# A recurrent mixer with its score blocks stored head innermost, turned by fours, and multiplied on 128 rows

## The chip, the cores and the metric

The program runs on one core of a Trainium2 chip. The core has five engines that work from queues of their own: TensorE (PE in the profile; the loads of its stationary operand are listed as PEld), VectorE (DVE), ScalarE (ACT), GpSimd (POOL) and SyncE (SP), which issues the transfers here. The metric is the device time in microseconds (us) of one execution, and its median over the runs.

## The reference, cut to what matters

The reference is a block of four parts in a row (a gated mixer, a recurrent mixer, a second mixer with attention, and feed-forward layers between them) on 256 tokens of width 1024. The change touches the recurrent mixer alone, which has 16 heads of 64:

```python
kk = heads(k * k_k)
kk = kk / jnp.maximum(jnp.sqrt(jnp.sum(kk * kk, axis=-1, keepdims=True)), 1e-12)
k = k * (1 + (a - 1) * k_a)
...
y = wkv7_scan(rh, decay, kh, vh, -kk, kk * ah)

def step(state, inp):
    r_t, w_t, k_t, v_t, a_t, b_t = inp
    sa = jnp.einsum('bhvk,bhk->bhv', state, a_t)
    state = (state * w_t[:, :, None, :] + sa[..., None] * b_t[:, :, None, :]
             + v_t[..., None] * k_t[:, :, None, :])
    return state, jnp.einsum('bhvk,bhk->bhv', state, r_t)
...
bonus = jnp.sum(rh * kh * r_k.astype(f32), axis=-1, keepdims=True) * vh
y = (y + bonus.reshape(bsz, seq, d)).astype(h.dtype)
return (y * g) @ w_o, v_first
```

## The kernel before, in words

The recurrence over 256 tokens is done in four chunks of 64 tokens. For each chunk `c` and head there is a 128x128 block of scores: the rows are the chunk's tokens seen through `b` and `k` (`BK`), the columns are its tokens seen through `a` and `r` (`AR`). `scores(c, g)` computes eight heads' blocks (`g` is the half of the heads) with TensorE into two banks, one for even heads (`sce`) and one for odd ones (`sco`), and VectorE multiplies them by a mask into `SC[g]`. `SC[g]` holds, on 128 partitions, 32 blocks (four chunks by eight heads) by 2 halves (`x`: 0 for the `a` columns, 1 for the `r` columns) by 64 columns, in this order: a block's columns lie side by side.

Within a chunk the first 64x64 part `A` of each block has to be inverted as a triangular system. It is split in 32x32 blocks. `by_problems(g)` turns the two diagonal blocks of each problem with 128 small matmul instructions against an identity (`turn`, bank `rb`), so that `Ab` has one problem per partition (128 problems: 2 halves, 2 diagonal blocks, 32 chunk-and-head pairs) and the 32x32 numbers of it along the row. `Ab` is divided by the squared norms of the keys. These are summed by TensorE (`squares`, bank `ssps`, 16 rows by 256 tokens), and `norms()` moves them with 16 transfers on SP's queue to `pd`, one problem per partition; their reciprocal is `ip`. `solve(s)`, 31 steps on VectorE, computes the inverses into `Xb`. `Ab` and `Xb` are the two halves of the tile `ABX`.

The inverses go back in two forms: into `SC` (bank `xt`, `turn` on 64 rows) and into `X1` (bank `x1`, `turn` on 32 rows). Then come 64 products of 32x32 with 32 rows each (bank `q`), copied into `X1`, and 64 more of 32x32 (bank `x21`), copied into the corner of each block of `SC`. The trace writes some names without their digits: the rows of `x` with `cstt,ABX` are `x1`, those with `SC,X` are `x21`, and `X` is `X1`.

The loop over the chunks then multiplies with these blocks: `removals` (bank `W`), `U`, the state's update `S` and the output `Y`. Each of `W`, `U` and `Y` takes one head's 64 columns of `SC` as the stationary operand; even heads go to the upper and odd heads to the lower 64 rows of the bank. `UV` holds the results on its upper 64 partitions and the values `v`, shifted by their mean (`ms`, `mv`, added by POOL), on the lower 64.

Beside this, on TensorE, there are the products for the values (`values`, bank `v`, `v0` and `v1` for the two halves of the columns, eight steps each), for the gates (`gates`, bank `g`), the turns of `BK` (`by_tokens`, bank `bkt`), the coefficients of the bonus (`coefs`, bank `cf`, 128 columns loaded and 2 streamed), the turn of the bonus (`bonus`, bank `bon`) and of the gates (`gate_turn`, bank `gt`).

A framework allots the buffers, places the waits and chooses the order on each engine from the order of the program, priorities and its own estimate of times. So TensorE's order is not always that of the source: a `v` step can stand ahead of a turn that was written before it. Every matmul of 32-bit floats appears in the trace as two instructions with a load each; the counts below are of instructions.

Of the kernel before, what the change touches and what calls it, by code (L numbers as in the profile page):

```python
# [9 lines left out]
F32 = mybir.dt.float32  # L10
# [48 lines left out]
for _n, _c in _PVL:  # L59
# [6 lines left out]
    ("ident", 128), ("ones", 128), ("onec", 1), ("bones", 128), ("invf", 1), ("hind", 128),  # L66
# [9 lines left out]
def consts():  # L76
# [13 lines left out]
    hi = np.zeros((P, 8, 16), np.float32)  # L90
    for m in range(8):
        hi[p, m, 2 * m + p // 64] = 1.0
    put("hind", hi.reshape(P, 128))
# [169 lines left out]
class Kern:  # L263
# [96 lines left out]
    def turn(self, out, a, rows):  # L360

        self.mm(out, a, self.cst("ident", 128)[rows, rows])

# [9 lines left out]
    def busy(self, n):  # L373

        o = self.cst("ones", 128).bitcast(BF16)
        ps = self.bank("busy")
        for _ in range(n):
            self.mm(ps[:, 0:T], o[:, 0:P], o)

# [373 lines left out]
    def rwkv(self, sums, nxt):  # L753
# [147 lines left out]
        ssps = []  # L901
# [21 lines left out]
        def squares(j, sq):  # L923
            if not ssps:
                ssps.append(self.bank("ssps"))
            for m in range(2):
                mm = 2 * j + m
                self.mm(ssps[0][0:16, 0:T], self.cst("hind", 128)[:, mm * 16:(mm + 1) * 16], sq[:, m, :], mm == 0, mm == 7)

        pd = self.tiny("pd", [P, 32], tag="pd")  # L930

        def norms():
            ss = self.mid("ss16", (16, T))
            self.ts(ss, ssps[0][0:16, 0:T], 1e-24, 2.0, ALU.max, ALU.mult)
            for b in range(2):
                for g in range(2):
                    for c in range(4):
                        p0 = 64 * g + 32 * b + 8 * c
                        nc.sync.dma_start(out=pd[p0:p0 + 8, :],
                                          in_=ss[8 * g:8 * g + 8, c * 64 + b * 32:c * 64 + b * 32 + 32])  # L940
# [25 lines left out]
        SC = [pair("SC")[:, 0:4096].rearrange("p (i x t) -> p i x t", i=32, x=2) for _ in range(2)]  # L966
        tri = self.cst("tri", 128)

        def scores(c, g):
# [6 lines left out]
            for par in range(2):  # L976
                o = SC[g][:, 8 * c + par:8 * c + 8:2, :, :].rearrange("p a x t -> p a (x t)")
# [12 lines left out]
        def by_problems(g):  # L990

            for e in range(2):
                ps = self.bank("rb")
                for i in range(16):
                    for b in range(2):
                        q = slice(32 * b, 32 * b + 32)
                        self.turn(ps[q, i * 32:(i + 1) * 32], SC[g][q, :, 0, 32 * b + 16 * e + i], q)
# [1112 lines left out]
```

## Time and profile before

| | |
|---|---|
| median of 3 runs | 1151.2 us (1149.26 to 1152.41) |
| the profiled execution | 1150.61 us, span of its instructions 1148.8 us |
| mean granted TensorE clock | 0.974 |
| TensorE busy | 1098.6 us (96%), 9220 matmul instructions |
| VectorE busy | 852.0 us (74%) |
| ScalarE busy | 574.9 us (50%) |
| POOL busy | 188.5 us (16%) |
| read from memory | 199.98 MB, 175 GB/s over the span |

The span runs from the first to the last instruction of the core. An engine is busy while one of its instructions runs; matmuls overlap each other, so their durations add up to more than the time they take together. The granted clock is a share of TensorE's full 2.4 GHz. The recurrent mixer lies at about 270 to 480 us of the span.

### The profile page before, as it was taken

The page shows a single profiled execution, that of the slowest core. Times are in us where ns is not written, and L with a number is a line of the kernel's source. Part 1 is how long each engine was busy: PE and PEld are TensorE (multiplying, and loading weights), DVE is VectorE, ACT ScalarE, POOL GpSimd, SP SyncE. Part 2 cuts the span into 40 slices and gives each one's busy share as a digit, 9 for nine tenths or more (in the row PEclk, how much of TensorE's full clock was granted, in tenths as well). Part 3 has the DMA queues.
Part 4 walks back from the last instruction along what each step waited for, and adds up shares of the span by engine and source line. Part 5 has one row for each costly group of instructions (what it writes and reads, how often), then busy time and mean ns, then how long its engine had stood idle before and what let it go on. Part 6 is the DMA issues. An engine that isn't in the chain of part 4 may idle for free. (4 is left out here: it accounts for less than half of the span.)

```text
span 1148.8 us, 22642 instructions
## 1 busy us (share of the span) xinstructions
PE 1098.6 (96%) x9220; PEld 1032.4 (90%) x9220; DVE 852.0 (74%) x1552; ACT 574.9 (50%) x922; POOL 188.5 (16%) x137
## 2 busy tenths in 40 slices
PE   9799999999999999999999998899899997999997
PEld 7699999999887598999999998897798997999886
DVE  6878988547954846888975579799886958965444
ACT  5565444444731545654454546454545654755342
POOL 1310000002010021110000004776363014000000
PEclk9999999999998979999999999899899998999999
DMA  8468887653441310588865543444144542555552
GB/s 291 152 206 306 302 297 281 209 183 126 136 142 59 132 38 21 184 302 314 281 206 184 182 164 130 151 164 132 67 135 157 172 162 92 179 186 169 187 189 82
DMA packets 57817, 202.52 MB, mean 176 GB/s; under 512 B 6896, under 2 KB 8560, under 8 KB 57712
## 3 DMA queue, kind: packets, MB, share of 16 engines
q1 hardware_dynamic: 57712, 201.07, 51.7%
q8 instruction: 72, 1.18, 0.4%
q14 instruction: 33, 0.27, 0.1%
HBM read 199.98 MB, written 1.05 MB: 175 GB/s over the span
## 5 line engine op out<-in xcount | busy, mean ns | idle before, releaser
L185 ACT ACTIVATE hi<-raw 128x1024 fp32r<-128x1024 f32 (+1 forms) x310 | 322.5, 1048 | 265.2 <-PE ps L355 175.2
L186 DVE TENSOR_TENSOR lo<-raw,hi 128x1024 fp32r<-128x1024 f32 (+1 forms) x258 | 315.4, 1226 | 145.3 <-ACT hi L185 144.9
L355 PE MATMUL ps<-xl,hi 128*128 128x256 f32 x1104 | 313.9, 285 | 4.1 <-DVE xl L343 4.1
L355 PE MATMUL ps<-xh,hi 128*128 128x256 f32 x1104 | 316.1, 287 | 1.4 <-ACT hi L185 1.0
L355 PE MATMUL ps<-xh,lo 128*128 128x256 f32 x1104 | 311.8, 283 | 2.8 <-DVE lo L186 1.5
L355 PEld LDWEIGHTS ps<-xl,hi 128*128 128x128 f32 x1104 | 210.4, 191 | 5.4 <-DVE xl L343 5.0
L355 PEld LDWEIGHTS ps<-xh,lo 128*128 128x128 f32 x1104 | 210.3, 191 | 4.4 <-DVE lo L186 3.0
L355 PEld LDWEIGHTS ps<-xh,hi 128*128 128x128 f32 x1104 | 209.7, 190 | 3.5 <-ACT hi L185 2.3
L186 POOL TENSOR_TENSOR lo<-raw,hi 128x1024 fp32r<-128x1024 f32 x52 | 126.0, 2442 | 115.6 <-ACT hi L185 75.9
L343 DVE SCALAR_TENSOR_TENSOR cva<-up,cwh,cva 128x256 f32<-128x256 f32 x232 | 103.3, 483 | 3.2 <-ACT cva L352 1.1
L355 PE MATMUL ps<-zl,hi 128*128 128x256 f32 x352 | 99.6, 283 | 0.0
L355 PE MATMUL ps<-zh,lo 128*128 128x256 f32 x352 | 99.4, 282 | 0.0
L355 PE MATMUL ps<-zh,hi 128*128 128x256 f32 x352 | 98.7, 280 | 0.0
L254 POOL TENSOR_TENSOR sq<-sq 128x512 f32<-128x512 f32 x17 | 23.3, 1374 | 453.2 <-ACT sq L352 453.0
L343 DVE SCALAR_TENSOR_TENSOR ada<-ada,cb 128x1024 f32<-128x1024 f32 x48 | 58.6, 1222 | 16.7 <-DMA ada<-in_ada_dram 16.6
L355 PEld LDWEIGHTS ps<-zh,hi 128*128 128x128 f32 x352 | 66.9, 190 | 0.0
L355 PEld LDWEIGHTS ps<-zh,lo 128*128 128x128 f32 x352 | 66.1, 188 | 0.0
L355 PEld LDWEIGHTS ps<-zl,hi 128*128 128x128 f32 x352 | 65.8, 187 | 0.0
L355 PE MATMUL ps<-hi,zl 128*128 128x256 f32 (+1 forms) x160 | 56.1, 350 | 0.0
L355 PE MATMUL ps<-hi,zh 128*128 128x256 f32 (+1 forms) x160 | 56.0, 350 | 0.0
L355 PE MATMUL ps<-lo,zh 128*128 128x256 f32 (+1 forms) x160 | 55.9, 350 | 0.0
L352 ACT ACTIVATE s<-z 128x256 f32<-128x256 f32 x44 | 18.3, 417 | 71.2 <-DVE z L340 71.1
(438 smaller groups left out, 2260.8 us busy)
## 6 DMA issues: line engine op xcount, KB each, us to landing
raw<-in_w_dram SPq DMA_DIRECT2D x325, 512.0 KB
ada<-in_ada_dram SPq DMA_DIRECT2D x48, 512.0 KB
h<-in_x_dram SPq DMA_DIRECT2D x8, 128.0 KB
cb<-in_c_dram SPq DMA_DIRECT2D x2, 512.0 KB
out_dram<-ht SPq DMA_DIRECT2D x3, 256.0 KB
raw<-in_w_dram SPq DMA_DIRECT2D x2, 256.0 KB
cstt<-in_cst_dram SPq DMA_DIRECT2D x1, 448.5 KB
poolw<-in_poolw_dram SPq DMA_DIRECT2D x1, 256.0 KB
```

What stands on the lines that cost most here:

```text
L185: self.nc.scalar.activation(out=hi[:, s], in_=raw[:, s], func=AF.Copy)
L186: eng.tensor_tensor(out=lo[:, s], in0=raw[:, s], in1=hi[:, s].bitcast(F32), op=ALU.subtract)
L254: e.tensor_tensor(out=self.parts[0], in0=self.parts[0], in1=self.parts[-1], op=ALU.add)
L343: self.nc.vector.scalar_tensor_tensor(out=out, in0=a, scalar=s, in1=b, op0=op0, op1=op1, **k)
L352: self.nc.scalar.activation(out=out, in_=a, func=f, **k)
L355: self.nc.tensor.matmul(out=out, lhsT=lhsT, rhs=rhs, start=start, stop=stop, skip_group_check=True)
```

## The change

The scores are stored in another order, `SC[g]` as 2 halves by 64 columns by 32 chunk-and-head pairs, so that the pairs are innermost. `by_problems` then turns four columns by 32 pairs at a time, with 128 rows and 128 columns, into one bank. `squares` adds its sums straight into the layout of `pd`, with 32-column windows of a constant (`hwin`), so that `norms()` and its transfers go. `Ab` is divided in two halves, each after its own turn. The inverses are turned by `first_block` (into `X1`) and by `blocks` (both diagonal blocks, by fours). `below` and `corner` are the two rounds of products, now with all 128 rows (zeros in `X1` and in the new tile `Q` fill the rest) and two heads at a time into different rows of one bank. Half of the steps of `v1` are placed between these rounds; before, all came ahead of them. The sums, the copies and the bonus of the first half of `v` move ahead of them. The second `corner` round, the turns of the bonus (`bonus_turn`) and of the gates move into the loop over the chunks. The first `removals` uses only the lower 64 rows. Eight matmuls without use (`busy_on`) are added ahead of the last normalised turn.

```diff
@@ -87,10 +87,9 @@
     put("invf", invf[p % 32][:, None])
-    hi = np.zeros((P, 8, 16), np.float32)
-    for m in range(8):
...
+    hi = np.zeros((P, 64), np.float32)
+    hi[p, 32 + p // 64] = 1.0
+    put("hwin", hi)
     s = (p % 64)[:, None]
@@ -376,6 +371,12 @@
             self.mm(ps[:, 0:T], o[:, 0:P], o)
+    def busy_on(self, n, src):
+        ps = self.bank("busy")
+        for _ in range(n):
+            self.mm(ps[:, 0:P], self.cst("ones", 128), src)
@@ -921,23 +922,19 @@
         def squares(j, sq):
-            if not ssps:
-                ssps.append(self.bank("ssps"))
+            if not pdps:
+                pdps.append(self.bank("pd"))
             for m in range(2):
                 mm = 2 * j + m
-                self.mm(ssps[0][0:16, 0:T], self.cst("hind", 128)[:, mm * 16:(mm + 1) * 16], sq[:, m, :], mm == 0, mm == 7)
+                for b in range(2):
+                    q = 64 * (mm // 4) + 32 * b
+                    for c in range(4):
+                        o = 8 * c + 2 * (mm % 4)
+                        self.mm(pdps[0][q:q + 32, 0:32], self.cst("hwin", 64)[:, 32 - o:64 - o],
+                                sq[:, m, 64 * c + 32 * b:64 * c + 32 * b + 32], mm % 4 == 0 and c == 0, mm % 4 == 3 and c == 3)
...
         pd = self.tiny("pd", [P, 32], tag="pd")
-        def norms():
-            ss = self.mid("ss16", (16, T))
...
@@ -963,7 +960,7 @@
-        SC = [pair("SC")[:, 0:4096].rearrange("p (i x t) -> p i x t", i=32, x=2) for _ in range(2)]
+        SC = [pair("SC")[:, 0:4096].rearrange("p (x t i) -> p x t i", i=32, x=2) for _ in range(2)]
         tri = self.cst("tri", 128)
@@ -974,7 +971,7 @@
             for par in range(2):
-                o = SC[g][:, 8 * c + par:8 * c + 8:2, :, :].rearrange("p a x t -> p a (x t)")
+                o = SC[g][:, :, :, 8 * c + par:8 * c + 8:2].rearrange("p x t a -> p a (x t)")
                 iv = pss[par].rearrange("p (a t) -> p a t", a=4)
@@ -989,17 +986,21 @@
-            for e in range(2):
-                ps = self.bank("rb")
...
+            ps = self.bank("rb")
+            for b in range(2):
+                for e in range(8):
+                    o = 32 * b + 4 * e
+                    self.mm(ps[:, b * T + 32 * e:b * T + 32 * e + 32],
+                            SC[g][:, 0, o:o + 4, :].rearrange("p t h -> p (t h)"), self.cst("ident", 128)[:, 32 * b:32 * b + 32])
+            for q in range(4):
+                for b in range(2):
+                    p0 = 64 * g + 32 * b
+                    o = Ab[p0:p0 + 32, q:32:4, :]
+                    iv = ps[32 * q:32 * q + 32, b * T:b * T + T].rearrange("p (a s) -> p a s", a=8)
+                    if g == 1 and q % 2:
+                        nc.vector.tensor_copy(out=o, in_=iv)
+                    else:
+                        self.act(o, iv, AF.Copy)
@@ -1011,12 +1012,14 @@
                     self.mm(ps[:, 16 * tt + 2 * m:16 * tt + 2 * m + 2], rk[:, m, tt * P:(tt + 1) * P],
-                            self.cst("hind", 128)[:, 0:2])
+                            self.cst("hwin", 64)[:, 32:34])
             self.act(cf.rearrange("p a b -> p (a b)"), ps[:, 0:32], AF.Copy)
...
+        bos = {}
         def bonus(n):
...
-            bo = self.hlp.tile([P, 2, 512], F32, tag=("hi", "lo")[n], name="bo")
+            bo = bos[n] = self.hlp.tile([P, 2, 512], F32, tag=("hi", "lo")[n], name="bo")
             for tt in range(2):
@@ -1025,12 +1028,15 @@
                     self.act(bo[:, tt, q], psv[tt][n][:, q], AF.Copy, scale=cf[:, tt, hh:hh + 1])
+        def bonus_turn(n):
             for j in (2 * n, 2 * n + 1):
...
                         o = (m % 2) * T + tt * P
-                        self.tr(ps[:, o:o + P], bo[:, tt, (m % 4) * P:(m % 4 + 1) * P], P)
+                        self.tr(ps[:, o:o + P], bos[n][:, tt, (m % 4) * P:(m % 4 + 1) * P], P)
                 for m in (2 * j, 2 * j + 1):
@@ -1106,15 +1112,20 @@
         scores(1, 1)
-        norms()
+        self.ts(pd, pdps[0][:, 0:32], 1e-24, 2.0, ALU.max, ALU.mult)
+        nc.vector.reciprocal(out=ip, in_=pd)
+        nc.vector.tensor_copy(out=Xb.rearrange("p a b -> p (a b)")[:, 0:1024:33], in_=ip)
         scores(2, 1)
...
             rkk(j)
-        nc.vector.reciprocal(out=ip, in_=pd)
-        nc.vector.tensor_copy(out=Xb.rearrange("p a b -> p (a b)")[:, 0:1024:33], in_=ip)
+        def divided(g):
+            q = slice(64 * g, 64 * g + 64)
+            self.tt(Ab[q], Ab[q], ip[q].unsqueeze(2).to_broadcast([64, 32, 32]), ALU.mult)
+        divided(0)
         by_problems(1)
-        self.tt(Ab, Ab, ip.unsqueeze(2).to_broadcast([P, 32, 32]), ALU.mult)
+        divided(1)
         for s in range(31):
@@ -1151,74 +1162,110 @@
         coefs()
-        for i in range(8):
-            next(v1)
...
         self.dump("Xb", ABX)
...
             nc.gpsimd.memset(u[0:64, :, :], 0.0)
-        def copied(o, iv, g):
-            if g == 0:
+        ms, mv = self.tiny("ms", [P, 2, 16], tag="cf", bufs=3), self.tiny("mv", [P, 4, 16], tag="mv", bufs=1)
+        def means(n):
+            for tt in range(2):
+                nc.vector.tensor_reduce(out=ms[:, tt, 8 * n:8 * n + 8], in_=psv[tt][n].rearrange("p (a b) -> p a b", a=8),
+                                        axis=AX.X, op=ALU.add)
+        def upper(n):
+            for c in range(4):
+                o, iv = UV[c // 2][64:128, c % 2, n * 512:(n + 1) * 512], psv[c // 2][n][64 * (c % 2):64 * (c % 2) + 64, :]
+                self.act(o, iv, AF.Copy)
+        def copied(o, iv, e):
+            if e % 2 == 0:
                 nc.vector.tensor_copy(out=o, in_=iv)
...
-        X1 = self.xp.tile([64, 2, 32, 32], F32, tag="xl", name="X1")
-        for e in range(4):
+        X1 = self.xp.tile([P, 2, 32, 32], F32, tag="xl", name="X1")
+        nc.gpsimd.memset(X1, 0.0)
+        block = lambda b: self.cst("ident", 128).rearrange("p (g b h) -> p b g h", g=2, b=2)[:, b]
+        by_col = lambda ps, q: ps[32 * q:32 * q + 32, :].rearrange("p (e a) -> p a e", e=8)
+        def first_block():
+            ps = self.bank("x1")
+            for e in range(8):
+                for q in range(4):
+                    self.mm(ps[32 * q:32 * q + 32, 64 * e:64 * e + 64], Xb[:, :, 4 * e + q], block(0))
+            for q in range(4):
+                copied(X1[0:32, :, :, q:32:4].rearrange("p g h e -> p (g h) e"), by_col(ps, q), q)
+        def blocks(b):
             ps = self.bank("xt")
-            for i in range(8):
+            for e in range(8):
+                self.mm(ps[:, 64 * e:64 * e + 64], Xb[:, 4 * e:4 * e + 4, :].rearrange("p t s -> p (t s)"), block(b))
+            return ps
+        def blocks_out(b, ps):
+            for q in range(4):
                 for g in range(2):
-                    self.turn(ps[32 * g:32 * g + 32, i * 64:(i + 1) * 64], Xb[64 * g:64 * g + 64, 8 * e + i, :], slice(64 * g, 64 * g + 64))
-            for b in range(2):
...
+                    copied(SC[g][32 * b:32 * b + 32, 0, 32 * b + q:32 * b + 32:4, :],
+                           ps[32 * q:32 * q + 32, :].rearrange("p (e g h) -> p g e h", e=8, g=2)[:, g], g)
+        Q = {}
+        rows = lambda par: slice(64 * par, 64 * par + 64)
+        def below(cp):
+            ps = self.bank("q")
+            for i in range(16):
+                for par in range(2):
+                    g, ch = i // 8, 16 * cp + 2 * (i % 8) + par
+                    self.mm(ps[64 * par + 32:64 * par + 64, 32 * i:32 * i + 32], SC[g][:, 0, 32:64, ch], X1[:, g, ch, :])
+            for par in range(2):
+                copied(Q[0][32:64, :, 16 * cp + par:16 * cp + 16:2, :],
+                       ps[64 * par + 32:64 * par + 64, :].rearrange("p (g a t) -> p g a t", g=2, a=8), par)
+        def corner(cp):
+            ps = self.bank("x21")
+            for i in range(16):
+                for par in range(2):
+                    g, ch = i // 8, 16 * cp + 2 * (i % 8) + par
+                    self.mm(ps[64 * par:64 * par + 32, 32 * i:32 * i + 32], Q[0][:, g, ch, :], SC[g][:, 0, 32:64, ch])
             for g in range(2):
-                ps = self.bank("q")
-                for i in range(16):
...
+                for par in range(2):
+                    copied(SC[g][0:32, 0, 32:64, 16 * cp + par:16 * cp + 16:2].rearrange("p t a -> p a t"),
+                           ps[64 * par:64 * par + 32, T * g:T * g + T].rearrange("p (a t) -> p a t", a=8), par)
+        for i in range(4):
+            next(v1)
+            if i == 1:
+                bonus(0)
+                upper(0)
+                means(0)
+        first_block()
+        xt = [blocks(b) for b in (1, 0)]
+        Q[0] = self.slot("Q", (P, 2, 32, 32))
+        nc.gpsimd.memset(Q[0], 0.0)
+        blocks_out(1, xt[0])
+        next(v1)
+        next(v1)
+        below(0)
+        next(v1)
+        below(1)
+        next(v1)
+        blocks_out(0, xt[1])
+        corner(0)
+        means(1)
         for c in range(4):
             self.act(mv[64:128, c, :], ms[64 * (c % 2):64 * (c % 2) + 64, c // 2, :], AF.Copy, scale=-1.0 / 64)
-        for c in range(4):
-            for n in range(2):
...
+        upper(1)
         for c in range(4):
...
         bonus(1)
-        gate_turn()
@@ -1275,10 +1321,12 @@
             pss = [self.bank("W") for _ in range(2)]
+            q = slice(64, P) if c == 0 else slice(0, P)
             for g in range(2):
                 for i, par in ips:
-                    self.mm(pss[g][rows(par), vcol(i)], SC[g][:, 8 * c + 2 * i + par, 0, :],
-                            UV[c // 2][:, c % 2, vcol(8 * g + 2 * i + par)], i == 0, c == 0)
+                    self.mm(pss[g][rows(par), vcol(i)], SC[g][q, 0, :, 8 * c + 2 * i + par],
+                            UV[c // 2][q, c % 2, vcol(8 * g + 2 * i + par)], i == 0, c == 0)
             return pss
@@ -1305,7 +1353,7 @@
                     for i, par in ips:
-                        self.mm(ps[rows(par), vcol(i)], SC[g][:, 8 * c + 2 * i + par, 0, :], W[:, 8 * g + 2 * i + par, :])
+                        self.mm(ps[rows(par), vcol(i)], SC[g][:, 0, :, 8 * c + 2 * i + par], W[:, 8 * g + 2 * i + par, :])
                     copy_out(uvh, g, ps)
@@ -1319,6 +1367,8 @@
                         self.tt(o, iv, dcb, ALU.mult)
+            if c == 0:
+                corner(1)
             if c < 3:
@@ -1328,7 +1378,7 @@
                 for i, par in ips:
-                    self.mm(ps[rows(par), vcol(i)], SC[g][:, 8 * c + 2 * i + par, 1, :], uv[:, vcol(8 * g + 2 * i + par)],
+                    self.mm(ps[rows(par), vcol(i)], SC[g][:, 1, :, 8 * c + 2 * i + par], uv[:, vcol(8 * g + 2 * i + par)],
                             c == 0 and i == 0, True)
@@ -1341,7 +1391,11 @@
                 self.act(sq[g][y0:y0 + 64], o, AF.Square)
+            if c == 0:
+                bonus_turn(0)
+                bonus_turn(1)
             if c == 1:
+                gate_turn()
                 gn(0, sq, (nc.gpsimd, nc.gpsimd))
@@ -1366,6 +1420,7 @@
             if m == 6:
+                self.busy_on(8, sq[1][:, 0:P])
                 gated(0)
...
             gated(j)
```

## Rows read from the trace of the kernel before

**Rows 1.** Stretches: length, busy us (count) of PE, PEld, DVE, ACT, POOL; clock; DMA.
```profile
365.00:372.00 7.00, 7.00 (x58) 6.94 (x53) 0.00 (x0) 0.59 (x1) 0.00 (x0) 0.53 0.27 89
372.00:387.00 15.00, 15.00 (x91) 11.03 (x89) 14.40 (x72) 6.27 (x13) 0.00 (x0) 1.00 0.41 135
...
401.70:410.80 9.10, 8.26 (x257) 7.63 (x256) 6.23 (x13) 6.50 (x17) 8.59 (x6) 1.00 0.37 126
...
412.00:426.00 14.00, 14.00 (x237) 13.58 (x233) 2.73 (x4) 3.91 (x8) 0.00 (x0) 0.52 0.01 2
426.00:452.20 26.20, 25.77 (x673) 23.17 (x672) 17.45 (x45) 14.01 (x35) 1.63 (x2) 1.00 0.07 22
452.20:460.80 8.60, 5.59 (x49) 5.13 (x45) 7.37 (x19) 6.70 (x16) 5.22 (x6) 0.97 0.02 5
460.80:464.00 3.20, 3.20 (x16) 3.20 (x17) 3.08 (x10) 1.50 (x4) 0.00 (x0) 0.55 0.58 164
```

**Rows 2.** Timeline of PE: start us, duration us, instructions, count.
```profile
362.07 3.87 PE L355 MATMUL rb<-cstt,SC 32*32 32x32 f32 x128
365.88 7.38 PE L355 MATMUL g<-raw,xg 128*128 128x160 f32 x32
373.09 1.04 PE L358 MATMUL bkt<-cstt,BK 128*128 128x128 f32 x8
...
383.46 3.63 PE L355 MATMUL cf<-cstt,rk 128*128 128x2 f32 x32
386.95 7.11 PE L355 MATMUL v<-raw,xv 128*128 128x512 f32 x16
393.90 1.04 PE L358 MATMUL bon<-cstt,bo 128*128 128x128 f32 x8
394.77 7.03 PE L355 MATMUL v<-raw,xv 128*128 128x512 f32 x16
...
410.83 5.70 PE L355 MATMUL q<-X,SC 32*32 32x32 f32 x125 [0.87 <-DVE X L1167]
...
423.27 1.97 PE L358 MATMUL bon<-cstt,bo 128*128 128x128 f32 x8
...
426.02 1.20 PE L355 MATMUL W<-UV,SC 128*64 128x64 f32 x32
...
433.46 1.11 PE L355 MATMUL U<-W,SC 128*64 128x64 f32 x31
```

**Rows 3.** Timeline of DVE around the solve, 372 to 397.
```profile
372.06 0.35 DVE L1114 RECIPROCAL ip<-pd 128x32 f32<-128x32 f32 x1 [7.26 <-DMA raw<-in_w_dram]
372.52 0.20 DVE L1115 COPY ABX<-ip 128x32 f32<-128x32 f32 x1
372.91 1.22 DVE L340 TENSOR_TENSOR ABX<-ABX,ip 128x1024 f32<-128x1024 f32 x1 [0.19 <-issue]
...
396.79 0.19 DVE L340 TENSOR_TENSOR ABX<-ABX,tb 128x31 f32<-128x31 f32 x1
```

**Rows 4.** Groups by line and form, 322 to 480: busy us, mean ns, idle before.
```profile
L340 DVE TENSOR_TENSOR SC<-sce,cstt 128x512 f32<-128x512 f32 x8 | 5.5, 686 | 9.3 <-PE sco L355 9.3
...
L1167 DVE COPY SC<-xt 32x256 f32<-32x256 f32 x8 | 3.3, 412 | 1.8 <-ACT SC L352 1.3 <-PE xt L355 0.3
```

**Rows 5.** Stretch of tile q alone: PE, PEld, DVE, ACT, clock, DMA.
```profile
411.00:412.00 1.00, 1.00 (x37) 1.00 (x35) 0.00 (x0) 0.00 (x0) 1.00 0.06 16
```

**Rows 6.** Loads of four tiles: ns min/median/max, first and last start us.
```profile
L355 PEld LDWEIGHTS rb<-cstt,SC x256: 127/145/148, 348.5 to 365.7; 32*32 32x32 f32 x128
...
L355 PEld LDWEIGHTS xt<-cstt,ABX x128: 102/107/107, 401.7 to 408.7; 64*32 64x32 f32 x128
...
L355 PEld LDWEIGHTS q<-X,SC x128: 101/152/153, 410.8 to 416.4; 32*32 32x32 f32 x128
...
L355 PEld LDWEIGHTS U<-W,SC x128: 132/138/138, 427.3 to 448.4; 128*64 128x64 f32 x128
```

**Rows 7.** Timeline of POOL, 400 to 411.
```profile
402.84 7.48 POOL L1219 TENSOR_TENSOR UV<-UV,mv 64x1024 f32<-64x1024 f32 x4
```

More of the change, by code (lines that the diff above doesn't have):

```diff
@@ L65 @@
 _CL = [
-    ("ident", 128), ("ones", 128), ("onec", 1), ("bones", 128), ("invf", 1), ("hind", 128),
+    ("ident", 128), ("ones", 128), ("onec", 1), ("bones", 128), ("invf", 1), ("hwin", 64),
     ("tri", 128), ("reset", 256), ("perm", 128), ("cmask", 128),
@@ L358, in tr @@
         self.nc.tensor.transpose(out, a, self.cst("ident", 128)[p0:p0 + n, p0:p0 + n])
-    def turn(self, out, a, rows):
-        self.mm(out, a, self.cst("ident", 128)[rows, rows])
     def warm(self):
@@ L900, in rwkv @@
         kps = {}
-        ssps = []
+        pdps = []
         def keys(j):
@@ L990, in by_problems @@
         def by_problems(g):
-            for e in range(2):
-                ps = self.bank("rb")
-                for i in range(16):
-                    for b in range(2):
-                        q = slice(32 * b, 32 * b + 32)
-                        self.turn(ps[q, i * 32:(i + 1) * 32], SC[g][q, :, 0, 32 * b + 16 * e + i], q)
-                o = Ab[64 * g:64 * g + 64, 16 * e:16 * e + 16, :].rearrange("p a b -> p (a b)")
-                if e == 0 and g == 1:
-                    nc.vector.tensor_copy(out=o, in_=ps[0:64, :])
-                else:
-                    self.act(o, ps[0:64, :], AF.Copy)
+            ps = self.bank("rb")
[13 more added lines that the diff above has]
+                        self.act(o, iv, AF.Copy)
         ip = self.tiny("ip", [P, 32], tag="pd")
@@ L1153, in rwkv @@
         coefs()
-        for i in range(8):
-            next(v1)
-            if i == 3:
-                bonus(0)
         self.dump("Xb", ABX)
@@ L1169, in copied @@
                 self.act(o, iv, AF.Copy)
-        X1 = self.xp.tile([64, 2, 32, 32], F32, tag="xl", name="X1")
-        for e in range(4):
-            ps = self.bank("xt")
-            for i in range(8):
-                for g in range(2):
-                    self.turn(ps[32 * g:32 * g + 32, i * 64:(i + 1) * 64], Xb[64 * g:64 * g + 64, 8 * e + i, :], slice(64 * g, 64 * g + 64))
-            for b in range(2):
-                for g in range(2):
-                    copied(SC[g][32 * b:32 * b + 32, :, 0, 32 * b + 8 * e:32 * b + 8 * e + 8],
-                           ps[32 * g:32 * g + 32, :].rearrange("p (i b c) -> p b c i", i=8, b=2)[:, b], g)
-            if e % 2 == 0:
-                ps1 = self.bank("x1")
-            for i in range(8):
-                for g in range(2):
-                    o = (8 * (e % 2) + i) * 32
-                    self.turn(ps1[32 * g:32 * g + 32, o:o + 32], Xb[64 * g:64 * g + 32, :, 8 * e + i], slice(64 * g, 64 * g + 32))
-            if e % 2:
-                for g in range(2):
-                    copied(X1[0:32, g, :, 8 * e - 8:8 * e + 8], ps1[32 * g:32 * g + 32, :].rearrange("p (i c) -> p c i", i=16), g)
@@ L1190, in rwkv @@
-        for e in range(2):
-            for g in range(2):
-                ps = self.bank("q")
-                for i in range(16):
-                    ch = 16 * e + i
-                    self.mm(ps[32:64, i * 32:(i + 1) * 32], SC[g][0:32, ch, 0, 32:64], X1[0:32, g, ch, :])
-                copied(X1[32:64, g, 16 * e:16 * e + 16, :].rearrange("p a b -> p (a b)"), ps[32:64, :], g)
-        ms, mv = self.tiny("ms", [P, 2, 16], tag="cf", bufs=3), self.tiny("mv", [P, 4, 16], tag="mv", bufs=1)
-        for tt in range(2):
-            for n in range(2):
-                nc.vector.tensor_reduce(out=ms[:, tt, 8 * n:8 * n + 8], in_=psv[tt][n].rearrange("p (a b) -> p a b", a=8),
-                                        axis=AX.X, op=ALU.add)
+        X1 = self.xp.tile([P, 2, 32, 32], F32, tag="xl", name="X1")
@@ L1265, in rwkv @@
         vcol = lambda hh: slice(hh * 64, (hh + 1) * 64)
-        rows = lambda par: slice(64 * par, 64 * par + 64)
         ips = [(i, par) for i in range(4) for par in range(2)]
```

18 lines of the change are left out of this document (removed).

## The prediction

> **What bounds the kernel now.** I read the page first (TensorE is busy through nearly the whole span, so a microsecond counts only if it leaves TensorE's queue), then the recurrent mixer, 320 to 480 us, as a table of stretches, then TensorE's order of work in it, and last the tiles that the change touches. The table shows where the queue is slow rather than full [rows 1]: in 365 to 372 and in 412 to 426 TensorE is busy all the time, at a granted clock of 0.53 and 0.52, so almost wholly at 1.2 of 2.4 GHz. Before the clock fell it did the same both times, matmuls of 32x32: the turn of the score blocks `rb`, and the rounds that begin with `q` [rows 2]. In the mixer's loop, 426 to 452.2, the clock is full and TensorE is busy 25.8 of 26.2 us. VectorE does nothing at all in 365 to 372: the reciprocal waits 7.3 us for the squared norms, which come in 16 small transfers [rows 1, 3].
>
> **The turn of the score blocks (`by_problems`).** Removed: 128 instructions per call, 3.8 us from `rb` to the next row. Added: 32 per call, each with a load of 128 columns and 32 columns streamed. The nearest row is `cf`, 128 loaded and 2 streamed: 32 in 3.63 us, the last one's tail taken off 0.109 each, so 3.5 us [rows 2]. Two calls: -0.6. The copies become eight per call, 256 numbers each. The second call's eight, four on each engine at about 0.41 [rows 4], add 0.9 us before the solve on VectorE, not on TensorE's path.
>
> **The clock behind it.** `g`, 32 instructions of 160 columns, took 7.2 us to the next start at the lower clock. `v` streams 512 columns in 0.434 us at the full one (16 in 6.95 us to the next start), so 160 take 0.136 and the 32 take 4.35 [rows 2]: -2.85 if the clock stays up, 0 if not. I take the whole: `cf`, also long loads with little streaming, ran at 1.00 [rows 1].
>
> **The squared norms.** Removed: 16 instructions of 256 columns (0.217 each by `v`, 3.5 us) and 16 transfers. Added: 128 of 32 columns. `q` shows such instructions in one column group at the full clock: 35 loads of about 0.10 us touch 1.00 us [rows 5], so 0.032 each, 4.1 us: +0.6. SP's queue loses these issues, and the weight loads behind them move up; TensorE has no gap there that waits for one, so nothing.
>
> **The solve.** Without the transfers it waits for the second turn alone: matmuls to about 366, copies to 367.4, the division 1.2 us, start about 368.6 instead of 374.1. It took 22.8 us to 397.0 with the other work in between [rows 3], so it ends about 391.4. TensorE, 2.85 earlier, has four of the eight steps of `v1` done at about 391. Before, `v1` hid 5 us of slack behind the solve; now the blocks are wanted in its middle. It is a tie: +0.5, bounds 0 and 5.6.
>
> **Blocks by 128 rows.** From 401.7 to 410.8 the `xt` and `x1` turns take 9.1 us, 0.84 of it idle [rows 1]. They become 64 instructions with 32 strided columns in four column groups, and 32 with long loads. The latter take 32 x 0.109 = 3.5. For the former, a strided load decides. `rb` reads every 128th number: its load lasts 145 ns, against 107 for `xt` and 101 for the shortest `q`, also 32 columns but contiguous [rows 6]. Its instructions start every 28.8 ns in two row groups (128 in 3.87 us less the last one's 0.22 [rows 2]), 57.6 per group, where one group of `q` needs 32. So 32 strided columns occupy a group for at most 57.6 ns. Four groups side by side give 14 ns per instruction, two 28.8: 0.9 to 1.8 us, taken 1.4. Sum 4.9 for 9.1: -4.2.
>
> **`q` and corner rounds.** 12.45 us from 410.83 to 423.27 [rows 2] become 256 instructions in two column groups at 28.8 ns: 7.35, at the full clock since they stand between steps of `v1`. -5.1; at half clock up to +2.25. The second corner round (1.85) only moves into the loop.
>
> **Turns moved into the loop.** `bon` took 0.87 at 393.9, `bon` and `gt` 2.75 from 423.27 at the lower clock [rows 2]. 20 instructions at 0.109 are 2.2: -1.4. ScalarE's eight copies of `bon` move with them, among copies of the loop; nothing for them, as ScalarE is busy 14 of 26.2 us there [rows 1].
>
> **The shift of V on POOL.** It took 7.5 us in four parts under the block turns [rows 7]. Now the sums over the second half come after the last step of `v1`, with only one corner round (1.85) left to hide two sums, the copies and the first part of 1.9: about 5 in all, 3 uncovered, two of them filled by the moved turns: +1.0, bounds 0 and 3.
>
> **Strided scores in the loop.** `W`, `U` and `Y` load 64 columns of `SC`, now 32 numbers apart: 384 instructions. Now they start every 29.6 ns (31 in 1.11 us less the last one's 0.22 [rows 2]) in two column groups, set by the 64 columns streamed. No row shows 64 strided columns. Below: 0, if the load stays under the streaming. Above, `rb`'s 57.6 per 32 makes 115 per group and 57.6 per instruction: 28 x 384 = +10.75. I take the upper, because the load itself lasts a third longer, less 2 us that the loop's slack absorbs (672 instructions x 29.6 ns = 19.9 of 26.2 us): +8.75.
>
> Strided writes I cost at nothing: the copy of 32 numbers 33 apart took 0.20 us, an operation on 31 contiguous ones 0.19 [rows 3]. The Trainium skill, Advanced Engine Details and Errata, SBUF Cachelines, says that accesses which each fall on another 16-byte line pay a penalty. On the load of weights `rb` agrees (145 against 107 ns); VectorE's write does not (0.20 against 0.19), and the measurement decides. By the rule the 16 score products of 0.68 us [rows 4] would grow too, up to 10.9 us if doubled, and the sum would come out near 1157.
>
> **The added matmuls (`busy_on`).** 16 instructions of 0.109, 1.75 us, stand where TensorE waits for the last normalisation (3 of the 8.6 us up to 460.8 are idle). They are hidden; without that cover they cost 1.75. Behind, 460.8 to 464 ran at 0.55 [rows 1]: at most 1.45 to win, taken -1.0.
>
> **Sum.** -0.6 - 2.85 + 0.6 + 0.5 - 4.2 - 5.1 - 1.4 + 1.0 + 8.75 - 1.0 = -4.3. The profiled execution took 1150.6 (span 1148.8 and 1.8 around it), 0.6 under the median 1151.2; so 1146.3 for the like of it, 1146.9 for the median. I write 1146.5.
>
> **Rivals.**
> Loads hidden: strided loads of 64 columns fit under the streaming, the 8.75 go: about 1138. For it: 57.6 is only an upper bound from `rb`. Against: its load lasts longer, at the same clock.
> Column groups collide: the two groups of `W`, `U`, `Y` read the same 128 partitions, `rb`'s two different ones. If their strided loads can't run side by side, each instruction takes 115 instead of 57.6 ns: 384 x 57.6 = +22, and the `q` rounds, 128 x 28.8, +3.7: about 1172. It turns the sign from 70 ns per instruction on (28 + 4.3/0.384 = 39 more than 29.6). Against: contiguous loads of two column groups do overlap (29.6 for 64 columns each).
> Solve late: TensorE waits at the first block for the whole 5.6 us instead of 0.5: about 1152. For it: the tie above, and any weight split that VectorE takes up within the solve.
> Clock stays low: `g` and the `q` rounds at 1.2 GHz: +2.85 + 5 = about 1154. For it: long loads with little streaming may count less than `v`. Against: `cf` at 1.00.
> Strided writes cost double: the 16 score products hold up the two turns and the solve: 1157. For it: 32 numbers are a short test. Against: 0.20 and 0.19.
>
> **Chances.** The sum 0.39, loads hidden 0.25, columns collide 0.13, solve late 0.11, clock low 0.08, writes 0.04. 0.3% (3.5 us) is what a measurement of this kernel can tell from no change. The sum's own range is 1142 to 1151, from the bounds of the solve and of POOL: three quarters of it faster, the rest same. Faster 0.29 + 0.25 + 0.04 (a little late) = 0.58; same 0.10 + 0.07 + 0.02 (part of the low clock) = 0.19; slower 0.13 + 0.06 + 0.04 = 0.23. The range of 8 in 10 reaches from hidden loads to the low clock: 1137 to 1156; colliding columns and doubled writes are left out.
>
> **What the next profile would show.** The clock in 365 to 372 and from the last step of `v1` to the first `W` is 1.00; `g` takes 4.4 us. No transfer to `pd`, no wait of the reciprocal; the solve starts at 368 to 369. First `W` about 411 instead of 426. Loads of `W`, `U`, `Y` longer than 138 ns [rows 6], starts near 57 ns apart; the loop 36 to 39 us. I am wrong if the loop keeps its 26 us and the moved pieces (faster), if it passes 45 (slower), or if TensorE idles ahead of the first block.

## The result and the profile after

| | before | after |
|---|---|---|
| median of 4 runs | 1150.24 us (1149.26 to 1152.41) | 1161.31 us (1158.44 to 1162.01) |
| ratio, 95% interval | | 1.0089 (1.0065 to 1.0113) |
| the profiled execution | 1150.61 us, span 1148.8 | 1158.44 us, span 1156.7 |

The changed kernel is 11 us slower by the medians, 10 by the ratio; 1146.5 was forecast. The ratio sets a kernel's runs against runs of the kernel before made beside them, and goes before the medians here; the difference of two ratios is uncertain by some 0.003, or 3.5 us. The two profiled executions don't run in step (this one is nearly 2 us early at the end of the k matmuls), so what counts is the length of a stretch, not its place.

The table of stretches of the changed kernel, columns as in [rows 1]:

```profile
359.97:362.93 2.96, 0.00 (x2) 0.00 (x1) 2.90 (x4) 0.00 (x0) 0.00 (x0) 0.93 0.46 173
362.93:369.80 6.87, 6.87 (x33) 6.87 (x33) 0.00 (x0) 0.00 (x0) 0.00 (x0) 0.50 0.02 4
369.80:375.70 5.90, 5.90 (x34) 5.90 (x35) 3.85 (x10) 1.49 (x4) 0.00 (x0) 0.75 0.17 42
...
415.70:461.10 45.40, 45.23 (x820) 41.60 (x819) 21.88 (x52) 21.77 (x49) 5.86 (x5) 1.00 0.04 14
...
470.00:473.00 3.00, 3.00 (x25) 2.82 (x24) 3.00 (x10) 1.89 (x4) 0.00 (x0) 1.00 0.40 147
```

The loop, from the first `W` to the first `yt`, takes 45.4 us at the full clock and with hardly any idle; it was 26.2 [rows 1], and 45 was the length from which the prediction called itself wrong. Well ahead of it stands a stretch that the kernel before did not have: TensorE idle for 2.96 us while VectorE works.

TensorE's timeline, the stretch of the second `by_problems` and pieces of the blocks and the loop:

```profile
357.99 1.98 PE L354 MATMUL v<-raw,xv 128*128 128x512 f32 x4
362.93 7.04 PE L354 MATMUL rb<-cstt,SC 128*128 128x32 f32 x32 [2.96 <-DVE SC L339]
369.78 6.06 PE L354 MATMUL g<-raw,xg 128*128 128x160 f32 x32
375.67 1.04 PE L357 MATMUL bkt<-cstt,BK 128*128 128x128 f32 x8
...
402.56 1.64 PE L354 MATMUL x<-cstt,ABX 128*32 128x64 f32 x64
404.13 3.79 PE L354 MATMUL xt<-cstt,ABX 128*128 128x64 f32 x32
...
411.44 4.15 PE L354 MATMUL q<-X,SC 128*32 128x32 f32 x128 [0.89 <-DVE SC L1185]
...
415.67 1.48 PE L354 MATMUL W<-UV,SC 64*64 64x64 f32 x20
417.08 2.06 PE L354 MATMUL x<-SC,Q 128*32 128x32 f32 x62
...
433.55 2.22 PE L354 MATMUL U<-W,SC 128*64 128x64 f32 x32
```

`rb` waits for VectorE's last score product, its 32 matmuls then take 7.04 us at a clock of 0.50, and `g` 6.06 for the 4.4 forecast. The first `W` comes at 415.67, not at 411. In the loop, 32 `U` start within 2.22 - 0.28 us, 62.6 ns apart (31 steps), where it was 29.6 [rows 2].

VectorE's timeline ahead of the second `by_problems`, first the last score product of the kernel before, then the changed kernel from half of the division on, and its last product:

```profile
361.34 0.68 DVE L340 TENSOR_TENSOR SC<-sco,cstt 128x512 f32<-128x512 f32 x1
```

```profile
356.35 1.21 DVE L339 TENSOR_TENSOR ABX<-ABX,ip 64x1024 f32<-64x1024 f32 x1
357.48 1.04 DVE L339 TENSOR_TENSOR SC<-sce,cstt 128x512 f32<-128x512 f32 x1
...
361.87 1.01 DVE L339 TENSOR_TENSOR SC<-sco,cstt 128x512 f32<-128x512 f32 x1
```

Before, the last product ended at 362.02 and `rb` began at 362.07 [rows 2]: whatever made the products later would make `rb` later. Now six of them stand one behind the other, from 357.48 to 362.88, and the division stands in front of them.

VectorE's score products and TensorE's weight loads in the changed kernel, ns as shortest/median/longest:

```profile
L339 DVE TENSOR_TENSOR SC<-sce,cstt x8: 1016/1048/1077, 335.7 to 361.0; 128x512 f32<-128x512 f32 x8
...
L354 PEld LDWEIGHTS U<-W,SC x128: 184/216/235, 420.0 to 455.5; 128*64 128x64 f32 x128
```

Same operation, same shape: 1048 ns for 686 [rows 4], and 216 ns for 138 [rows 6]. The first was forecast not to change, the second to grow.

### The profile page after: what moved, and what is told of

Read it like the earlier page. It is cut to its first block, busy times and chain, and to the rows that moved or that the text cites. A ratio compares the mean times of both kernels' runs of the same rounds, so it can differ in the third digit from the quotient of the medians.

```text
span 1156.7 us, 22193 instructions
## 1 busy us (share of the span) xinstructions
PE 1105.8 (96%) x8996; PEld 1041.3 (90%) x8996; DVE 860.4 (74%) x1558; ACT 581.1 (50%) x933; POOL 192.3 (17%) x139
## 5 line engine op out<-in xcount | busy, mean ns | idle before, releaser
L184 ACT ACTIVATE hi<-raw 128x1024 fp32r<-128x1024 f32 (+1 forms) x310 | 323.2, 1048 | 266.5 <-PE ps L354 171.4
```

The costliest lines, as they stand in the source:

```text
L184: self.nc.scalar.activation(out=hi[:, s], in_=raw[:, s], func=AF.Copy)
```

## The experiments

Theory A: the layout costs, at two places. The loads of 64 strided columns set the pace of `W`, `U` and `Y`; the strided writes hold back the second `by_problems`. Theory B: the layout is harmless, and the longer loop comes from the matmuls that were moved into it.

**e1_old_layout.** The whole change, but the scores lie as before, and `by_problems` turns them as before.

```diff
-SC = [pair("SC")[:, 0:4096].rearrange("p (x t i) -> p x t i", i=32, x=2) for _ in range(2)]
+SC = [pair("SC")[:, 0:4096].rearrange("p (i x t) -> p x t i", i=32, x=2) for _ in range(2)]
```

> The changed kernel with the scores stored as before (a head's 64 columns side by side) and with the old 32-row turns in by_problems, since the new ones need the new layout; all the rest of the change stays. Theory A (the layout costs: a strided 64-column weight load takes some 2 ns a column more, 35 ns for each of 384 matmuls of the token loop, and a strided score write takes 1.05 us for 0.69): the span from the first W matmul to the first yt transpose falls from 45.4 to about 32 us, the score products take 0.69 us again, and the time is about 1145 us (1141 to 1149). Theory B (the layout is harmless, the cost is in the rounds and turns that were moved into the loop and in front of it): the loop stays above 42 us and the time stays at 1158 to 1162.

1141.19 us, ratio 0.9931 (0.9906 to 0.9956): faster than either kernel. Its loop in the table of stretches:

```profile
416.45:448.20 31.75, 31.28 (x757) 27.68 (x757) 19.36 (x49) 19.14 (x47) 7.00 (x5) 0.95 0.07 20
```

31.75 us with the same moved matmuls in it, but for the first corner round (64 instructions), which lies ahead of the first `W` here. B falls: the layout with its turns costs 0.0158 of 1150, 18 us, and the rest of the change gains 8. TensorE's timeline at the places where the layout is used outside the loop:

```profile
362.11 1.98 PE L354 MATMUL v<-raw,xv 128*128 128x512 f32 x4
364.97 3.87 PE L354 MATMUL rb<-cstt,SC 32*32 32x32 f32 x128 [0.87 <-DVE SC L339]
...
375.45 1.04 PE L357 MATMUL bkt<-cstt,BK 128*128 128x128 f32 x8
...
409.29 2.27 PE L354 MATMUL q<-X,SC 128*32 128x32 f32 x128 [0.68 <-DVE SC L1185]
...
413.40 1.21 PE L354 MATMUL x<-SC,Q 128*32 128x32 f32 x64
416.45 1.15 PE L354 MATMUL W<-UV,SC 64*64 64x64 f32 x32 [1.85 <-POOL UV L1267]
```

From the `v` step to the first `bkt` it is 13.3 us, in the changed kernel 17.7: 4.3 us. The rounds read strided scores too: `q` takes 2.27 us for 4.15, a corner round (the rows of `x` with `SC,Q`) 1.21 for about 2.1, so with the second corner round 3.7 us in all. Of these, 1.85 stand here as a wait for POOL ahead of `W`, which the changed kernel does not have.

**e3_loop_reads.** The changed kernel with contiguous loads in the loop alone; it multiplies by other numbers.

```diff
-SC[g][:, 0, :, 8 * c + 2 * i + par], W[:, 8 * g + 2 * i + par, :]
+SF[g][:, lump(0, 8 * c + 2 * i + par)], W[:, 8 * g + 2 * i + par, :]
```

(`SF` is the flat buffer, `lump` 64 numbers side by side; `W` and `Y` likewise.)

> The changed kernel, whose W, U and Y matmuls load 64 columns that lie side by side in the score buffer (so they multiply by other numbers than the reference's; count and size are unchanged). Theory A: the loop falls from 45.4 to about 32 us and the time to 1146 to 1150; all ahead of the first W stays. Theory B (the loop is longer because of the corner, bonus and gate matmuls moved into it and of what they wait for): the loop stays above 42 us, 1158 to 1162.

1149.93 us, ratio 0.9999 (0.9980 to 1.0017): 0.0090 under the changed kernel, 10.4 us. Ahead of the first `W` nothing was changed, and the trace shows the gain in the loop, 45.4 - 34.8 = 10.6 us:

```profile
416.80:451.60 34.80, 33.82 (x821) 29.63 (x819) 21.45 (x52) 21.10 (x49) 5.26 (x5) 1.00 0.06 17
```

**e4_score_writes.** The other half: contiguous writes, strided loads.

```diff
-o = SC[g][:, :, :, 8 * c + par:8 * c + 8:2].rearrange("p x t a -> p a (x t)")
+o = SF[g][:, 1024 * c + 512 * par:1024 * c + 512 * par + 512].rearrange("p (a n) -> p a n", a=4)
```

> The changed kernel, whose score products are written as 512 numbers side by side (so every number stands in a wrong place, and the mask is scaled by 0.02 to keep the solve finite); the loop still loads strided columns. Theory A, its second part (the strided writes hold back the second by_problems): the products take 0.69 us, the TensorE idle of 3 us ahead of the second rb turns falls to under 1 us, the bkt transposes start 2 to 5 us earlier; 1155 to 1159. Rival (the writes lie beside other work, as the prediction priced them): 1160 to 1162.

1153.53 us, ratio 1.0024 (1.0005 to 1.0043): 0.0065 under the changed kernel, 7.5 us. Its timeline:

```profile
359.15 3.76 PE L354 MATMUL rb<-cstt,SC 128*128 128x32 f32 x32
362.74 6.27 PE L354 MATMUL g<-raw,xg 128*128 128x160 f32 x32
368.85 1.88 PE L354 MATMUL v<-raw,xv 128*128 128x512 f32 x4
```

VectorE's score products, ns, and when the first and the last start:

```profile
L339 DVE TENSOR_TENSOR SC<-sco,cstt x8: 670/679/682, 338.2 to 361.3; 128x512 f32<-128x512 f32 x8
```

The products take 0.68 us again, nothing is waited for ahead of `rb`, and the 32 turns take 3.76 us for 7.04. `g` is still slow. But the edit takes away more than the strides. `rb` reads the first 2048 numbers of the buffer, and written side by side the products of chunks 2 and 3 fall behind them, so `rb` no longer waits for the last four: it begins at 359.15, and the last product begins at 361.3. Where that wait is kept and the writes are contiguous, TensorE still idles 0.87 us (e1). So the 7.5 us are the strides and the wait together, and the 4.3 of e1's timeline are nearer to the writes alone. That 10.4 + 7.5 come close to the 18.2 that e1 gives back is in part chance: the removed wait is in them, and the rounds' 3.7 are not.

**e2_layout_alone.** The kernel before with the layout and nothing else.

```diff
-SC = [pair("SC")[:, 0:4096].rearrange("p (i x t) -> p i x t", i=32, x=2) for _ in range(2)]
+SC = [pair("SC")[:, 0:4096].rearrange("p (x t i) -> p i x t", i=32, x=2) for _ in range(2)]
```

> The kernel before, with nothing but the scores stored head innermost. Theory A: the stretch from the first W matmul to the first yt transpose grows from 26.2 to about 39.5 us (384 matmuls by 35 ns), the score products from 0.69 to 1.05 us; 1158 to 1168 us. Theory B: within 2 us of the kernel before, 1148 to 1153.

1162.90 us, ratio 1.0121 (1.0096 to 1.0145): +14 us. The loop takes 37.3 us for 26.2. There is a gain in it too: the old turns now load 32 columns that lie side by side, and 128 of them take 2.25 us, where the kernel before needed 3.87 [rows 2] (e9, below, 3.85 at a clock of 1.00).

```profile
361.39 2.25 PE L355 MATMUL rb<-cstt,SC 32*32 32x32 f32 x128 [1.81 <-DVE SC L340]
```

```profile
426.70:464.00 37.30, 37.16 (x673) 35.05 (x672) 18.06 (x45) 14.97 (x35) 2.04 (x2) 0.98 0.06 16
```

Here nothing but the writes was made slower ahead of `rb`, and TensorE idles 1.81 us for them, where the kernel before had no such wait. Behind that idle the turns ran at a clock of 0.96.

**p1_probe.** The disputed cost by itself, behind the loop of the changed kernel. One line of each kind, here for the distance 32:

```diff
+lhsT=FL[0][:, i % 32:2048:32], rhs=UV[1][:, 1, vcol(i // 2 % 8)]
+nc.vector.tensor_tensor(out=FL[1][:, 0:4096].rearrange("p (n a) -> p a n", a=32)[:, 0:4, :], in0=pin, in1=mk4, op=ALU.mult)
```

> The changed kernel with a probe behind its loop that changes no output: 32 matmuls of 64 stationary and 64 moving columns in two column groups, six times, with the stationary columns 1, 2, 4, 8, 16 and 32 numbers apart; then the score product (512 numbers out of PSUM times the mask) on VectorE, and a copy of 512 numbers out of PSUM on ScalarE, four times for each of the same six distances of the numbers written. Theory A (the layout's strides are what costs): 30 ns from start to start at distance 1 and 62 to 70 at 32; the product 0.69 us at distance 1 and 1.05 at 32. The Trainium skill, Advanced Engine Details and Errata, SBUF Cachelines, counts lines of 16 bytes: by it the price is reached at distance 4 and doesn't grow from there. Rival (what costs in the loop is which buffer is read beside which writes): no difference between the six beyond 10%.

TensorE's timeline (each matmul has two records), and groups of VectorE and ScalarE. Distances 1, 2, 4, 8, 16, 32 are L1408 to L1418 on TensorE, L1422 to L1432 on VectorE, L1434 to L1444 on ScalarE:

```profile
465.20 2.09 PE L1408 MATMUL prb<-UV,SC 128*64 128x64 f32 x64
467.11 2.09 PE L1410 MATMUL prb<-UV,SC 128*64 128x64 f32 x64
469.03 4.00 PE L1412 MATMUL prb<-UV,SC 128*64 128x64 f32 x64
472.87 4.01 PE L1414 MATMUL prb<-UV,SC 128*64 128x64 f32 x64
476.71 3.77 PE L1416 MATMUL prb<-UV,SC 128*64 128x64 f32 x64
480.32 3.99 PE L1418 MATMUL prb<-UV,SC 128*64 128x64 f32 x64
```

```profile
L1426 DVE TENSOR_TENSOR SC<-prb,cstt 128x512 f32<-128x512 f32 x4 | 4.2, 1056 | 0.0
...
L1432 DVE TENSOR_TENSOR SC<-prb,cstt 128x512 f32<-128x512 f32 x4 | 4.1, 1024 | 0.0
...
L1422 DVE TENSOR_TENSOR SC<-prb,cstt 128x512 f32<-128x512 f32 x4 | 2.8, 691 | 12.7 <-PE prb L1418 12.6
L1424 DVE TENSOR_TENSOR SC<-prb,cstt 128x512 f32<-128x512 f32 x4 | 2.8, 691 | 0.1
```

```profile
L1444 ACT ACTIVATE SC<-prb 128x512 f32<-128x512 f32 x4 | 4.7, 1181 | 0.0
...
L1438 ACT ACTIVATE SC<-prb 128x512 f32<-128x512 f32 x4 | 4.4, 1098 | 0.0
...
L1436 ACT ACTIVATE SC<-prb 128x512 f32<-128x512 f32 x4 | 2.6, 653 | 0.1
...
L1434 ACT ACTIVATE SC<-prb 128x512 f32<-128x512 f32 x4 | 2.4, 595 | 3.1 <-DVE SC L1432 3.1
```

On TensorE and VectorE the whole price is there at distance 4, 16 bytes, and up to 32 it stays within 7% of that; on ScalarE it is 1098 ns at 4 and 1181 at 32. At distance 2 nothing is paid on TensorE and VectorE (691 ns, as at 1). A record starts every 29.8 ns at distance 1 (1.91 us by 64) and every 60 at 4. The Trainium skill, Advanced Engine Details and Errata, SBUF Cachelines, has it so: lines of 16 bytes, and a penalty unless a line is hit at least twice. The probe agrees, writes included (distance 2 hits a line of 16 bytes twice, distance 4 once); the size is the probe's. With the probe in it the kernel took 1202.55 us, one run.

**e5_filled.** The changed kernel with the idle ahead of the second `by_problems` filled.

```diff
 divided(0)
+self.busy_on(14, SC[1][:, 0, 0:16, 8:16])
 by_problems(1)
```

> The changed kernel with 14 matmuls of 128 columns, whose result nobody reads, put between the last score matmuls and the second by_problems; they read scores of the third chunk pair, so they start near 359 and fill the idle 3 us ahead of the turns (the order of the work moves one step of v, 2 us, from in front of the gap to behind g). Theory A1 (the idle is what lets the clock fall, and the half clock is what makes 32 turns take 7.0 us and g 5.9): the clock stays at 1.00, rb and g take 3.8 and 4.4 us, and even with the v step behind them the first bkt comes some 3 us earlier; 1156 to 1159. Theory A2 (the clock falls on the long loads with 32 columns whatever stands ahead, or the idle alone costs): rb and g stay at 13 us together, and the v step behind them makes it 1161 to 1164.

1159.94 us, ratio 1.0089 (1.0066 to 1.0113): no gain. The clock held at first and fell in the middle of the turns:

```profile
361.74:365.20 3.46, 3.39 (x28) 3.20 (x28) 3.46 (x4) 0.00 (x0) 0.00 (x0) 1.00 0.02 5
365.30:369.80 4.50, 4.50 (x33) 4.50 (x33) 0.00 (x0) 0.00 (x0) 0.00 (x0) 0.78 0.00 0
369.80:376.60 6.80, 6.80 (x33) 6.80 (x34) 4.67 (x15) 1.49 (x4) 0.00 (x0) 0.64 0.16 46
```

The turns took 4.7 us for 7.04 (3.76 at the full clock), but `g` 7.0. A1 holds for the turns in part, A2 for the time. That the idle is what lets the clock fall is not shown: here it fell behind 3.4 us of work without a gap, and in e2 it stayed up behind 1.81 us.

**e6_squares_alone.** The kernel before with the norms in place.

```diff
-norms()
+self.ts(pd, pdps[0][:, 0:32], 1e-24, 2.0, ALU.max, ALU.mult)
+nc.vector.reciprocal(out=ip, in_=pd)
```

> The kernel before with the squared norms alone changed: summed in place by 128 small matmuls, no transfers to pd, the reciprocal early and the division in two halves. The prediction's terms: +0.6 for the matmuls, and the solve starts near 369 to 370 instead of 374.2; in this kernel the blocks come behind all of v1, so the earlier solve gives nothing: within 1 us of the kernel before. Rival (the end of the solve does set the blocks, and v1 is only pushed about): 1145 to 1148.

1150.68 us, ratio 1.0007 (0.9992 to 1.0022): nothing that can be measured. All 16 transfers are gone and the time is the same; the wait of the reciprocal [rows 3] was hidden. (That row names a load of weights as what ended the wait; in e2 and e10, with the same transfers, it is `pd`.) And the change puts a new wait where there was none:

```profile
362.96 3.87 PE L358 MATMUL rb<-cstt,SC 32*32 32x32 f32 x128 [0.88 <-DVE SC L343]
```

The reciprocal and half of the division now stand on VectorE ahead of the last six score products, and `rb` waits 0.88 us for them.

**e7_turns_back** and **e8_no_busy**, both from e1_old_layout.

```diff
 bonus(1)
+bonus_turn(0)
+bonus_turn(1)
+gate_turn()
...
-self.busy_on(8, sq[1][:, 0:P])
```

(The first three lines are e7, which leaves them out of the loop; the last is e8.)

> The version of e1_old_layout with the bonus and gate turns put back ahead of the loop. The prediction gave the move 1.4 us: so 1 to 3 us slower than e1_old_layout, 1142 to 1145. Rival (in the loop they hold up W and Y as much as they cost ahead of it, and TensorE is busy in both places): the same time as e1_old_layout, within 1 us.

> The version of e1_old_layout without the added matmuls of busy_on. The prediction gave them 1.0 us by the clock after the last normalisation: the clock falls to 0.5 for one stretch behind the loop and the time is 1 to 2 us over e1_old_layout. Rival (they lie in idle time and the clock would stay up without them, or they delay the last turns by as much as they save): within 0.7 us.

e7: 1142.91 us, ratio 0.9942 (0.9922 to 0.9962). e8: 1142.12 us, ratio 0.9931 (0.9908 to 0.9953). Beside e1's 0.9931 the move of the turns is worth 1.3 us and the added matmuls 0 by the middles; neither differs from nothing, nor from the forecast 1.4 and 1.0. In e8's profiled execution the tail ran at the full clock without the added matmuls:

```profile
453.70:458.00 4.30, 4.27 (x32) 3.90 (x33) 4.30 (x11) 1.91 (x4) 0.00 (x0) 1.00 0.24 98
```

It is alone in that. In the 3 us behind the last `yt` the clock was 1.00 in all six profiled executions that have these matmuls (the probe apart: the changed kernel, e1, e3, e4, e5, e7), and 0.50 to 0.58 in five of the six that don't (the kernel before, e2, e6, e9, e10). So these matmuls do go with a clock that stays up; what that is worth in time these runs can't tell from nothing.

**e9_g_ahead.** e8 with `g` in front of the second `by_problems`.

```diff
+for _ in range(4):
+    psg = next(ga)
 by_problems(1)
```

> The version of e8_no_busy (the change with the old layout and the old turns of by_problems, without the added matmuls) with the 32 g matmuls ahead of the second by_problems. Theory A1 (the half clock falls on whatever stands behind the second by_problems, and what it costs is g's length): g runs at the full clock in 4.4 us for 6.1 to 6.9, partly in the idle 0.9 us; against that the solve starts 3.5 us later; 1 to 3 us faster than e8_no_busy, 1138 to 1141. Theory A2 (the clock falls as early whatever stands there, or the later solve holds back the first block): the same as e8_no_busy or up to 3 us slower, 1141 to 1145.

1142.83 us, ratio 0.9930 (0.9907 to 0.9953): the same time as e8, though 1 to 3 us could hide in the intervals. `g` ran at the full clock in 4.6 us as A1 has it, and the turns too; the tail was slow, as in nearly all without the added matmuls:

```profile
361.85:366.40 4.55, 4.55 (x35) 4.38 (x33) 2.81 (x5) 0.00 (x0) 0.00 (x0) 1.00 0.21 51
366.40:370.20 3.80, 3.80 (x130) 3.76 (x129) 0.68 (x1) 2.15 (x5) 1.81 (x1) 1.00 0.60 219
...
452.00:458.00 6.00, 4.68 (x26) 4.25 (x25) 5.89 (x15) 3.25 (x5) 1.93 (x1) 0.72 0.28 87
```

**e10_rounds_alone.** The kernel before with the rounds on 128 rows (and the first `W` on 64, which goes with them) and nothing else of the change. Core of the diff:

```diff
-for i in range(8):
-    next(v1)
...
+first_block()
+xt = [blocks(b) for b in (1, 0)]
+blocks_out(1, xt[0])
+next(v1)
+next(v1)
+below(0)
```

> The kernel before with nothing but the rounds on 128 rows (first block, blocks, below and corner between the steps of v1, the second corner in the loop, the sums and the upper halves of UV early): old layout, old turns of by_problems, norms by 16 transfers, bonus and gate turns ahead of the loop, no added matmuls. The prediction's terms for it: -4.2 - 5.1 + 1.0 = -8.3, so 1142. With it the other parts together come to nothing, and the whole of the loss is the layout. Rival (the gain of the old-layout version comes as much from the norms and the moved turns): 1145 to 1148. And a third: with the transfers the solve ends late, the blocks in the middle of v1 wait for it, and the rounds alone give less than 3 us, 1147 to 1151.

1141.95 us, ratio 0.9928 (0.9912 to 0.9943): -8.3 us by the ratio, as forecast for its terms, and as fast as e1, e8 and e9. One part of the change holds the whole gain, as far as these runs can tell. TensorE ahead of the rounds, and the tail:

```profile
409.82 3.61 PE L358 MATMUL q<-X,SC 128*32 128x32 f32 x128 [2.82 <-DVE SC L1188]
```

```profile
454.20:461.00 6.80, 5.48 (x27) 5.41 (x27) 6.68 (x17) 2.90 (x5) 1.34 (x1) 0.50 0.25 77
```

In this execution `g`, in its old place behind the turns, ran at 1.00 (367.1 to 371.5).

## Why the prediction was wrong

**The step that failed** is "Strided writes I cost at nothing: the copy of 32 numbers 33 apart took 0.20 us, an operation on 31 contiguous ones 0.19". By the probe a number written 4 or more apart costs VectorE (1056 - 691) / 512 = 0.71 ns more. For 32 numbers that is 0.02 us, and the two rows compared are given to 0.01 and show two different operations: they could not tell the two cases apart. For 512 it is 0.36 us, and the last products stand one behind the other in front of a turn that had no slack. TensorE idles 1.81 us for that in e2; the stretch from the `v` step to the first `bkt` is 4.3 us longer than in e1, and e4, which takes a wait away too, gives back 7.5. The rival "strided writes cost double", 1157, had the mechanism, with a chance of 0.04; its price was too high for the writes alone (10.9), and it did not come alone.

**A wait that was not priced.** The early norms were given no place in VectorE's queue ahead of the score products. In e6 this alone makes `rb` wait 0.88 us; with e2's 1.81 it is most of the 2.96 us of the changed kernel.

**The clock behind `rb`** (-0.6 and -2.85) did not come. In the changed kernel the turns run at 0.50 behind the idle, and `g` takes 6.1 us. Without the strided writes, e4, the turns take 3.76 us, hardly less than the old ones' 3.87, and still `g` 6.3. In ten of the eleven profiled executions that have `g` behind the turns its clock was 0.53 to 0.75, with old turns and new; only e10 had 1.00. So the long loads were no cure. That `cf` ran at 1.00 was no ground for `g`: in the changed kernel `cf` had 1.00 again, `g` 0.75, and the `v` steps behind `cf` 0.87 (389.5 to 402.5).

**The strided loads of the loop** (+8.75) were right in kind and too low: 1.7 us by e3. The probe gives 60 ns per instruction, the prediction 57.6; in the loop it is 62.6, so 384 x 33 = 12.7 by the starts, where e3 measures 10.4. The rival "column groups collide" asked for 115 ns; the two groups do load side by side. "Loads hidden" is out. The other part of the loop's 45.4 us (36 to 39 forecast) is the first corner round, of which 62 of 64 instructions came behind the first `W`, 2.06 us that were counted ahead of it.

**The rounds on 128 rows** (-4.2 - 5.1 + 1.0 = -8.3) came out as forecast in e10, but that is in part luck. The forecast prices strided loads at 28.8 ns; the changed kernel's rounds need 31. In e10 the scores lie as before, and there such rounds need 16 (e1's `q`), while TensorE waits 2.82 us ahead of `q`, which was priced at nothing. First block and blocks took 1.64 + 3.79 us for the 4.9 forecast.

**The solve** (+0.5) was late for another reason than the one weighed: it started at 374.64 for 368.6, behind the copies of the late `rb`. It cost nothing that shows, since more of `v` went ahead of it: the first block, at 402.56, follows `v` with no idle. e6 and e10 agree: the early norms buy nothing.

**The squares, the moved turns, `busy_on`** (+0.6, -1.4, -1.0): +0.8, -1.3 and 0 by the middles of e6, e7 and e8, none of them beyond its interval, so none of the three terms is confirmed or refuted by a time.

The miss by the ratio is 10.2 + 4.3 = 14.5 us. An estimate from the figures above: 4.3 to 7.5 of writes, 3.45 of turn and clock, 1.65 of loads, and 1.85 of the rounds (3.7 less the wait that they fill) make 11 to 14.5; what is left is within the intervals. What stays open is where the clock falls in a given execution: e1 and e8 have the same instructions around the second `by_problems`, and `g` ran at 0.66 in one and at 0.72 in the other.

## What to carry to other kernels

A layout is paid where the data is used most: here the turns of the score blocks got a handier shape, and the loop's 384 loads, the rounds and 16 products a worse one. Before a cost is set to nothing, work out how large the effect would be in the row that is to exclude it; a row of 32 numbers cannot exclude a price per number. An experiment that moves where numbers are written can also change who waits for whom; look at the trace for that before its time is put down to one cause. And try the parts of a change one by one: one of them made this kernel 8 us faster, and one more than took it back.

## What was not expected of the hardware

The step between free and full price is sharp: distance 2 costs TensorE and VectorE nothing (30 and 691 ns), distance 4 all of it (60 and 1056 ns), 32 no more (the same 4.0 us for 64 records, and 1024). ScalarE pays most, 595 to 1098 ns for 512 numbers at 4 and 1181 at 32, and a little (653) already at 2.

Not only the loaded operand pays. A corner round streams 32 columns of the scores past a contiguous load (`x` with `SC,Q`): 64 instructions took 1.21 us with the columns side by side (e1), and 62 took 2.06 with the columns 32 numbers apart.

The 16 instructions of `busy_on`, put into a wait, went with a full clock behind it in six executions of six, and without them it was full in one of six (e8).
